# Start of a fused layer step: block 0's 1/rms from token rows, the first transfers in a new order, p's weights split once for two blocks

## The chip, the cores and the metric

The kernel runs on one core of one Trainium2 chip. The metric is the device time of one execution in microseconds (us), the median of three runs. The engines are TensorE (PE, with its weight loads as PEld), VectorE (DVE), ScalarE (ACT), GpSimd (POOL) and SyncE (SP). Each executes its own instructions strictly in the order in which they were built in; semaphores order the engines among themselves. SP, ACT and POOL issue DMA transfers.

## The reference, cut to what matters

One encoder layer over 2048 prompt tokens and 64 tokens of a sample stream, with model width 1024. Only what the start of the kernel computes is shown in full.

```python
h = rms_norm(x, g_pre)                       # x * 1/sqrt(mean(x*x) + 1e-6) * g_pre
proj = h @ w_in                              # 1024 -> ten groups of 1024
vA, bA, cA, zA, q, f, iv, zB, gA, gB = split_cols(proj)
...                                          # short convolution (path A), gated recurrence (path B)
merged = sigmoid(gA) * yA + sigmoid(gB) * yB
x = x + rms_norm(merged @ w_o, g_post)
gate = sigmoid(rms_norm(x, g_ple) @ w_ple_gate)
x = x + (p @ w_ple_proj) * gate              # p: 256 values per token
```

## The kernel before, in words

Activations lie feature-major: 128 features on the partitions, tokens along the free dimension. The 2112 tokens are worked on in three blocks of 704, each in two halves (`segs`) of 352.

A float32 product is put together from three matmuls of a rounded type. `split` (L183) makes the parts of a matrix: ScalarE casts it to the rounded type ("hi", L184), and VectorE subtracts that from the original ("lo", L185). Then hi by hi, hi by lo and lo by hi are added up in PSUM.

The projections go in groups of two column tiles (`sgroup`), each by a scheme of seven half-size products in place of eight. For it `combined` takes four weight tiles of `w_blk` (called A11, A21, A22, A12; 128x512, 256 KB each) and, in the first block, makes four sums and differences S3, S1, S2, S4 from them on VectorE (L281), splits A11, A12, A22 and the four sums, and stores low parts and sums in DRAM for later blocks. On the activation side `operands` (L604) takes x_fm rows in pairs, row i and row i+4, for i = 0 to 3 ("k"). It multiplies each with g_pre and 1/rms (L610), and makes seven operands from the pair by subtractions (L617, L618, L623, L624) and splits. The two first groups are those of `head_prep` for head 0: FF with QQ, then ZB with IV. `gates` (GA with GB) follows behind them.

`ple` computes p by w_ple_proj for one block. It goes over eight column tiles j, loads a piece of w_ple (128 KB), splits it, and does 12 matmuls of 128x352 (two halves, two row tiles of p, three parts). ScalarE copies each half out of PSUM (L922), and POOL's queue stores the tile. PSUM has three buffers for it. Pieces of weights share a pool: five buffers for raw tiles, four for hi, four for lo, three for sums. All larger activation tiles live in a ring of 52 slots of 128x704.

The start is in the last part of the program (L1078 to L1101). SP loads two tiles of p; POOL's queue loads the eight x_fm tiles and block 1's p; ScalarE's queue loads the small vectors. Then p is split; eight x_fm tiles are squared on ScalarE (L573, L576) and added up on VectorE (L577). `ple` of block 0 runs for six column tiles. 1/rms follows: column sums by matmuls with a column of ones (L558), scale and epsilon on VectorE (L530), the power -1/2 on POOL (L532), spreading over the partitions by matmuls with the identity (L542) and copies (L568). The rest of `ple`, the splits of block 1's p and the operands come next. Block 1's `ple` is handed to `gates` as a filler, two column tiles ahead of each of the four k steps of its first group.

The order on each engine is fixed when the program is built. The framework goes by program order and by a cost model; code under `tc.high_priority()` moves ahead of other work, and `tc.issue_after(ins)` holds what it covers back behind `ins`. A load that reuses a buffer waits for the readers of its former content.

Of the kernel before, what the change touches and what calls it, by code (L numbers as in the profile page):

```python
# [18 lines left out]
P = 128  # L19
# [63 lines left out]
def hybrid_step(  # L83
# [31 lines left out]
    def nm(s):  # L115
        uid[0] += 1
        return f"{s}_{uid[0]}"

    def rt(n=BN, dt=F32):
        t = ring.tile([P, BN + 4], dt, tag="r", name=nm("r"))  # L120
        return t if n is None else t[:, :n]
# [59 lines left out]


    def split(src, hi, lo):  # L183
        A.copy(hi, src)  # L184
        V.tensor_tensor(lo, src, hi.bitcast(F32), ALU.subtract)  # L185

    def split_rt(src):
        hi, lo = rt(dt=F32R), rt(dt=F32R)
        split(src, hi, lo)
        return hi, lo  # L190
# [34 lines left out]
    def load_w(idx):  # L225
# [5 lines left out]
                parts.append(split_w(raw, (idx, half_)))  # L231
        return parts

    last, hooks = [None], []

    def placed():
# [13 lines left out]
    def run(gen, n=None):  # L250
        for i, _ in enumerate(gen):
            if n is not None and i + 1 == n:
                break
# [17 lines left out]
    def combined(i1, i2, first, ahead):  # L271

        with tc.high_priority() if ahead else nullcontext():
            if not first:
                return {n: kept_w(i1, i2, n) for _, n, _, _, _ in PRODUCTS}
            a11, a21, a22, a12 = (load_raw(w_blk[i, h]) for i, h in ((i1, 0), (i2, 0), (i2, 1), (i1, 1)))
            out = dict(A11=split_w(a11, (i1, 0)))

            def total(name, x, y, op):
                s = sum_tile()  # L280
                V.tensor_tensor(s, x, y, op)  # L281
                out[name] = keep_sum(name, i1, s)
                return s

            total("S3", a11, a21, ALU.subtract)
            s1 = total("S1", a21, a22, ALU.add)
            s2 = total("S2", s1, a11, ALU.subtract)
            out["A12"] = split_w(a12, (i1, 1))
            out["A22"] = split_w(a22, (i2, 1))
            total("S4", a12, s2, ALU.subtract)  # L290
            return out
# [38 lines left out]
    def sgroup(i1, i2, hc, sink, first, mid=None, by_k=False, ahead=True, between=None):  # L330

        w = combined(i1, i2, first, ahead)
        ps, got = {}, {}

        def product(n, ks):
            bank, block, operand, start, _ = PRODUCTS[n]
            if bank not in ps:
                ps[bank] = ps_gemm()  # L340
            hi, lo = w[block]
            for k in ks:
                xhi, xlo = hc[operand][k]
                add = partial(T.matmul, ps[bank], skip_group_check=not start)
                add(hi[:, k, :], xhi, start=start and k == 0, stop=False)  # L345
                add(hi[:, k, :], xlo, start=False, stop=False)  # L346
                last[0] = add(lo[:, k, :], xhi, start=False, stop=k == KH - 1).ins  # L347

        if by_k:
            for k in range(KH):  # L350
                if between is not None:
                    between()
                for n in range(4):
                    product(n, (k,))
        for n, (bank, _, _, _, stop) in enumerate(PRODUCTS):
            if n >= 4 or not by_k:
                product(n, range(KH))
            if not stop:
                got[n] = hf()
                with tc.high_priority():  # L360
                    copied = A.copy(got[n], ps[bank])  # L361
                if n == 2 and mid is not None:
                    mid(copied.ins)
            if n == 3:
                u2 = got[0]
                V.tensor_tensor(u2, u2, ps["b"], ALU.add)
            elif n == 4:
                sink(0, 0, ps["a"], None)
            elif n == 5:
                sink(1, 0, u2, ps["c"])  # L370
                V.tensor_tensor(got[1], got[1], got[2], ALU.add)
                sink(1, 1, u2, got[1])
            elif n == 6:
                sink(0, 1, u2, ps["d"])
            hook()
# [186 lines left out]
    def rms(acc, out, segs):  # L562


        cols = [col_rstd(acc[:, cols_of(sg)], sg["n"]) for sg in segs]
        yield
        for sg, col in zip(segs, cols):
            A.copy(out[:, cols_of(sg)], spread(col, sg["n"]))  # L568
        yield

    def sum_squares(j, src, acc, n):
        if j == 0:
            A.activation(acc, src, AF.Square)  # L573
        else:
            sq = rt(n)
            A.activation(sq, src, AF.Square)  # L576
            V.tensor_tensor(acc, acc, sq, ALU.add)  # L577
# [23 lines left out]
                rstd_of(sc[:, 0:1], cols[:, i : i + 1], 1.0 / D)  # L601
            yield

    def operands(hc, rs, load):  # L604

        for i in range(KH):
            pair = []
            for k in (i, i + KH):
                xk = load(k)
                V.scalar_tensor_tensor(xk, xk, g_pre[:, k : k + 1], rs, ALU.mult, ALU.mult)  # L610
                pair.append(xk)
            (b11, b12), (b21, b22) = ([half(x, h) for h in range(2)] for x in pair)
            one = rt(dt=F32R)
            split(b11, half(one, 0), half(one, 1))
            hc["B11"].append((half(one, 0), half(one, 1)))
            s = rt()
            V.tensor_tensor(half(s, 1), b22, b12, ALU.subtract)  # L617
            V.tensor_tensor(half(s, 0), b12, b11, ALU.subtract)  # L618
            hi, lo = split_rt(s)
            hc["T3"].append((half(hi, 1), half(lo, 1)))  # L620
            hc["T1"].append((half(hi, 0), half(lo, 0)))
            t = rt()
            V.tensor_tensor(half(t, 0), b22, half(s, 0), ALU.subtract)  # L623
            V.tensor_tensor(half(t, 1), b21, half(t, 0), ALU.subtract)  # L624
            hi, lo = split_rt(t)
            hc["T2"].append((half(hi, 0), half(lo, 0)))
            hc["T4"].append((half(hi, 1), half(lo, 1)))
            hi, lo = split_rt(pair[1])
            hc["B21"].append((half(hi, 0), half(lo, 0)))
            hc["B22"].append((half(hi, 1), half(lo, 1)))  # L630
            yield
# [266 lines left out]


    def load_p(bl, queue):  # L900
        raws = [rt(), rt()]
        for k, raw in enumerate(raws):
            queue.dma_start(raw, p_fm[k * P : (k + 1) * P, bl["t0"] : bl["t0"] + BN])
        return raws

    def ple(bl, ph, kept):
        for j in range(KB):
            raw = wp.tile([P, 4, P], F32, tag="raw", name=nm("raw"), bufs=5)[:, :2, :]
            SP.dma_start(raw, w_ple[j])
            with tc.high_priority():  # L910
                hi = wp.tile([P, 4, P], F32R, tag="hi", name=nm("hi"))[:, :2, :]
                lo = wp.tile([P, 4, P], F32R, tag="lo", name=nm("lo"))[:, :2, :]
                split(raw, hi, lo)
            t = rt()
            for s in bl["segs"]:
                pp, c = ps_attn()[:, :HN], cols_of(s)
                for k, (xhi, xlo) in enumerate(ph):
                    T.matmul(pp, hi[:, k, :], xhi[:, c], start=k == 0, stop=False)
                    T.matmul(pp, hi[:, k, :], xlo[:, c], start=False, stop=False)
                    last[0] = T.matmul(pp, lo[:, k, :], xhi[:, c], start=False, stop=k == 1).ins  # L920
                with tc.high_priority():
                    A.copy(t[:, c], pp)  # L922
            kept["p", j] = spill("p", j)
            G.dma_start(kept["p", j], t)
            hook()
            yield
# [150 lines left out]

    kepts = [{} for _ in blocks]  # L1078
    ph = load_p(blocks[0], SP)
    A.dma_start(vec, vecs)  # L1080
    A.dma_start(hist_s, hist0)
    xs = []
    for k in range(KB):
        xs.append(rt())
        G.dma_start(xs[k], x_fm[k * P : (k + 1) * P, :BN])
    ph1 = load_p(blocks[1], G)
    ph = [split_rt(raw) for raw in ph]
    acc, rs = rt(), rt()
    for k, xk in enumerate(xs):
        sum_squares(k, xk, acc, BN)  # L1090
    first_ple, first_rms = ple(blocks[0], ph, kepts[0]), rms(acc, rs, blocks[0]["segs"])
    run(first_ple, 6)
    run(first_rms, 1)
    run(first_ple, 1)
    run(first_rms)
    run(first_ple)
    ph = [split_rt(raw) for raw in ph1]
    hc = new_operands()
    run(operands(hc, rs, lambda k: xs[k]))
    constants()  # L1100
    fills = gates(blocks[0], hc, kepts[0], True, steps(ple(blocks[1], ph, kepts[1]), 2))  # L1101
    for bi, bl in enumerate(blocks):
        first, kept = bi == 0, kepts[bi]
        segs = bl["segs"]
# [118 lines left out]
```

## Time and profile before

| | us |
|---|---|
| median of 3 runs (2727.76 to 2732.46) | 2730.09 |
| the profiled execution | 2728.34 |
| its span from first to last instruction | 2726.6 |
| mean granted TensorE clock in it | 0.987 of full speed |
| TensorE's first matmul | 13.30 |
| VectorE's first multiplication of x with 1/rms (L610) | 34.23 |
| first matmul of the first group (L345) | 37.78 |
| last matmul of block 0's ple | 35.58 (end) |
| block 1's ple, from and to | 97.69, 115.68 |

The page of the profile begins with the busy time of each engine. Below it the span is cut into 40 equal slices, each with the busy share in tenths, the granted TensorE clock (PEclk) and the DMA rate. Then come the DMA queues, the chain of work that ended last, and the costliest groups of instructions. The trace behind the page can be asked for a timeline (start, duration, engine, line, operation, tiles and shapes, and in brackets the idle time just before with the instruction that ended it), or for the busy time of each engine by stretch. "x3" on a row means that three instructions are drawn together. Engine times of one instruction overlap a little with the next, so spacing is shorter than duration.

### The profile page before, as it was taken

What the parts mean: (1) busy time and instruction counts of PE and PEld (TensorE: products, weight loads), DVE (VectorE), ACT (ScalarE), POOL (GpSimd) and SP (SyncE); (2) the same over time, 40 slices, a digit from 0 to 9 for tenths busy, and PEclk for the clock granted to TensorE, in tenths of its full rate; (3) what the DMA queues carried; (4) which work ended last, traced back from release to release, by engine and by line L of the source; (5) the groups of instructions that cost most, each with busy time, mean ns of one, the idle gap of its engine ahead of it and who ended that gap; (6) DMA issues with size and microseconds to landing.
All of it is one profiled execution on the core that took longest, in us unless ns stands there. A gap on an engine that the chain in (4) does not pass through costs nothing.

```text
span 2726.6 us, 47857 instructions
## 1 busy us (share of the span) xinstructions
PE 2646.6 (97%) x16736; PEld 2610.7 (96%) x16736; DVE 1721.8 (63%) x3327; ACT 1457.9 (53%) x2796; POOL 367.9 (13%) x684
## 2 busy tenths in 40 slices
PE   6999999999999999999999999999999999999998
PEld 5999999999999999999999999999999999999988
DVE  6788888899666643566645567554355554357864
ACT  4665565454324553566654556454466654445654
POOL 1000001100332211011111210021010010010022
PEclk7999999999999999999999999999999999999999
DMA  5767777898988898766789998598866678888878
GB/s 200 268 239 275 260 243 278 280 314 291 346 312 288 305 340 271 243 224 223 232 279 335 390 335 259 180 349 306 268 224 219 217 225 269 272 290 305 280 240 313
DMA packets 365681, 748.90 MB, mean 275 GB/s; under 512 B 44704, under 2 KB 48320, under 8 KB 365440
## 3 DMA queue, kind: packets, MB, share of 16 engines
q1 hardware_dynamic: 325728, 589.84, 64.9%
q0 software_dynamic: 39424, 155.96, 15.6%
q8 instruction: 132, 2.16, 0.3%
q14 instruction: 109, 0.89, 0.1%
q10 hardware_dynamic: 288, 0.05, 0.0%
HBM read 538.29 MB, written 207.37 MB: 273 GB/s over the span
## 4 chain that ended last, share of the span: by engine, by line
PE 78%; DMA 8%; DVE 4%; issue 4%; ACT 2%; POOL 1%; SPq 0%; DVEq 0%; POOLq 0%; ACTq 0%
PE pg L345 17%; PE pg L346 17%; PE pg L347 17%; PE pg L472 3%; PE pg L473 3%; PE pg L471 3%; PE pg L438 3%; PE pg L439 3%; PE pg L440 3%; DMA raw<-w_blk 2%; DMA raw<-S 1%; PE pa L826 1%; PE pa L862 1%; PE pa L864 1%; PE pa L816 1%
## 5 line engine op out<-in xcount | busy, mean ns | idle before, releaser
L345 PE MATMUL pg<-r,hi 128*128 128x352 f32 x3360 | 1115.1, 333 | 15.9 <-ACT r L184 5.9
L346 PE MATMUL pg<-r,hi 128*128 128x352 f32 x3360 | 1090.4, 325 | 5.0 <-DVE r L185 5.0
L347 PE MATMUL pg<-r,lo 128*128 128x352 f32 x2400 | 779.9, 325 | 4.8 <-DMA lo<-low 3.5
L215 ACT CAST hi<-raw 128x512 fp32r<-128x512 f32 x740 | 455.9, 619 | 589.7 <-PE pg L346 216.3
L345 PEld LDWEIGHTS pg<-r,hi 128*128 128x128 f32 x3360 | 634.8, 189 | 26.8 <-ACT r L184 8.9
L346 PEld LDWEIGHTS pg<-r,hi 128*128 128x128 f32 x3360 | 635.6, 189 | 9.6 <-DVE r L185 9.5
L347 PEld LDWEIGHTS pg<-r,lo 128*128 128x128 f32 x2400 | 454.0, 189 | 7.0 <-DMA lo<-low 4.7
L347 PE MATMUL pg<-r,s 128*128 128x352 f32 x960 | 310.5, 324 | 0.4 <-DMA s<-low 0.3
L472 PE MATMUL pg<-r,hi 128*128 128x352 f32 x896 | 291.9, 326 | 2.6 <-DVE r L185 2.3
L471 PE MATMUL pg<-r,hi 128*128 128x352 f32 x896 | 290.3, 326 | 1.8 <-ACT r L184 1.7
L473 PE MATMUL pg<-r,lo 128*128 128x352 f32 x728 | 237.5, 326 | 8.3 <-DVE lo L185 7.2
L184 ACT CAST r<-r 128x352 fp32r<-128x352 f32 (+2 forms) x294 | 162.8, 589 | 144.0 <-DVE r L962 43.3
L184 ACT CAST hi<-raw 128x512 fp32r<-128x512 f32 (+1 forms) x232 | 138.1, 597 | 181.2 <-PE pg L346 44.1
L185 DVE TENSOR_TENSOR r<-r,r 128x352 fp32r<-128x352 f32 (+2 forms) x294 | 183.6, 650 | 60.7 <-ACT r L184 60.0
L185 DVE TENSOR_TENSOR lo<-raw,hi 128x512 fp32r<-128x512 f32 (+1 forms) x232 | 152.2, 660 | 73.2 <-ACT hi L184 66.8
L438 PE MATMUL pg<-r,hi 128*128 128x352 f32 x560 | 182.6, 330 | 7.9 <-ACT r L184 7.9
L439 PE MATMUL pg<-r,hi 128*128 128x352 f32 x560 | 183.9, 330 | 0.9 <-DVE r L185 0.6
L347 PEld LDWEIGHTS pg<-r,s 128*128 128x128 f32 x960 | 180.4, 188 | 1.3 <-DMA s<-low 1.3
L472 PEld LDWEIGHTS pg<-r,hi 128*128 128x128 f32 x896 | 169.9, 190 | 4.5 <-DVE r L185 4.3
L184 ACT CAST hi<-s 128x512 fp32r<-128x512 f32 x160 | 98.8, 619 | 139.7 <-PE pg L346 137.0
L471 PEld LDWEIGHTS pg<-r,hi 128*128 128x128 f32 x896 | 169.6, 190 | 3.3 <-ACT r L184 2.9
L361 ACT COPY hf<-pg 128x352 f32<-128x352 f32 x360 | 158.3, 446 | 0.6
(327 smaller groups left out, 3991.7 us busy)
## 6 DMA issues: line engine op xcount, KB each, us to landing
raw<-w_blk SPq DMA_DIRECT2D x588, 256.0 KB, 4.0
lo<-low SPq DMA_DIRECT2D x422, 256.0 KB, 3.9
raw<-S SPq DMA_DIRECT2D x400, 256.0 KB, 4.0
low<-lo SPq DMA_DIRECT2D x344, 256.0 KB, 3.7
s<-low SPq DMA_DIRECT2D x318, 256.0 KB, 3.8
S<-s SPq DMA_DIRECT2D x160, 256.0 KB, 3.3
r<-x_fm POOLq DMA_DIRECT2D x40, 352.0 KB, 7.0
r<-w_blk POOLq DMA_DIRECT2D x48, 256.0 KB, 7.2
```

The costliest lines, as they stand in the source:

```text
L184: A.copy(hi, src)
L185: V.tensor_tensor(lo, src, hi.bitcast(F32), ALU.subtract)
L215: A.copy(hi, raw)
L345: add(hi[:, k, :], xhi, start=start and k == 0, stop=False)
L346: add(hi[:, k, :], xlo, start=False, stop=False)
L347: last[0] = add(lo[:, k, :], xhi, start=False, stop=k == KH - 1).ins
L361: copied = A.copy(got[n], ps[bank])
L438: add(hi[:, k, :], xhi, start=start and k == 0, stop=False)
L439: add(hi[:, k, :], xlo, start=False, stop=False)
L471: T.matmul(ps, hi[:, k % 4, :], xhi[:, c], start=k == 0, stop=False)
L472: T.matmul(ps, hi[:, k % 4, :], xlo[:, c], start=False, stop=False)
L473: last[0] = T.matmul(ps, lo[:, k % 4, :], xhi[:, c], start=False, stop=k == KB - 1).ins
```

## The change

* **1/rms of block 0** comes from token rows. Twelve tiles of x_tok (128 tokens by 512 features, 256 KB each) are loaded, three go with each of the first four column tiles of ple, and ScalarE squares each with a sum along its row. One addition on VectorE joins the two halves of a row. Scale, power and spreading follow on one 128x6 tile. The eight squares and seven additions of 128x704 and the column sums by matmuls go.
* **The first requests all stand on SP**: two tiles of p, w_ple 0 to 4, the twelve rows, x_fm in the order of the operands' pairs, then block 1's p. w_ple 5 to 7 are requested by POOL's queue.
* **p's splits** stand under high priority, ahead of those of w_ple.
* **w_ple's splits** are held in eight tiles of the ring (hi and lo side by side), and block 1's ple uses them instead of loading and splitting again.
* For the first five column tiles the second half is copied out of PSUM by VectorE instead of ScalarE.
* **`behind`** holds the weight splits and sums of the first group (FF with QQ) back behind the splits of block 1's p, and those of the second group behind the split of B21 at k=2 of the operands.
* The operands' first step (k=0) now stands ahead of the last column tiles of block 0's ple, and the splits of block 1's p behind these.

Lines of the changed kernel are some 3 to 43 further down than those of before.

```diff
@@ -181,8 +181,7 @@
 
 
     def split(src, hi, lo):
-        A.copy(hi, src)
-        V.tensor_tensor(lo, src, hi.bitcast(F32), ALU.subtract)
+        return A.copy(hi, src).ins, V.tensor_tensor(lo, src, hi.bitcast(F32), ALU.subtract).ins
 
     def split_rt(src):
         hi, lo = rt(dt=F32R), rt(dt=F32R)
@@ -231,6 +230,8 @@
                 parts.append(split_w(raw, (idx, half_)))
         return parts
 
+
+    behind = []
     last, hooks = [None], []
 
     def placed():
@@ -331,7 +332,10 @@
 
 
 
-        w = combined(i1, i2, first, ahead)
+        with ExitStack() as order:
+            for ins in behind.pop(0) if behind else ():
+                order.enter_context(tc.issue_after(ins))
+            w = combined(i1, i2, first, ahead)
         ps, got = {}, {}
 
         def product(n, ks):
@@ -601,7 +605,7 @@
                 rstd_of(sc[:, 0:1], cols[:, i : i + 1], 1.0 / D)
             yield
 
-    def operands(hc, rs, load):
+    def operands(hc, rs, load, marks=None):
 
         for i in range(KH):
             pair = []
@@ -625,7 +629,10 @@
             hi, lo = split_rt(t)
             hc["T2"].append((half(hi, 0), half(lo, 0)))
             hc["T4"].append((half(hi, 1), half(lo, 1)))
-            hi, lo = split_rt(pair[1])
+            hi, lo = rt(dt=F32R), rt(dt=F32R)
+            done = split(pair[1], hi, lo)
+            if marks is not None:
+                marks.append(done)
             hc["B21"].append((half(hi, 0), half(lo, 0)))
             hc["B22"].append((half(hi, 1), half(lo, 1)))
             yield
@@ -898,19 +905,34 @@
 
 
     def load_p(bl, queue):
-        raws = [rt(), rt()]
+        raws = [rt() for _ in range(2)]
         for k, raw in enumerate(raws):
             queue.dma_start(raw, p_fm[k * P : (k + 1) * P, bl["t0"] : bl["t0"] + BN])
         return raws
 
-    def ple(bl, ph, kept):
+    def load_ple(j, queue):
+        raw = wp.tile([P, 4, P], F32, tag="raw", name=nm("raw"), bufs=5)[:, :2, :]
+        queue.dma_start(raw, w_ple[j])
+        return raw
+
+    def ple(bl, ph, kept, raws=(), held=None, marks=None):
+
+
         for j in range(KB):
-            raw = wp.tile([P, 4, P], F32, tag="raw", name=nm("raw"), bufs=5)[:, :2, :]
-            SP.dma_start(raw, w_ple[j])
-            with tc.high_priority():
-                hi = wp.tile([P, 4, P], F32R, tag="hi", name=nm("hi"))[:, :2, :]
-                lo = wp.tile([P, 4, P], F32R, tag="lo", name=nm("lo"))[:, :2, :]
-                split(raw, hi, lo)
+            if held is not None and j in held:
+                hi, lo = held[j]
+            else:
+                raw = raws[j] if j < len(raws) else load_ple(j, G if held is not None else SP)
+                with tc.high_priority():
+                    if held is not None:
+                        both = rt(4 * P, F32R).rearrange("p (k c) -> p k c", c=P)
+                        held[j] = hi, lo = both[:, :2, :], both[:, 2:, :]
+                    else:
+                        hi = wp.tile([P, 4, P], F32R, tag="hi", name=nm("hi"))[:, :2, :]
+                        lo = wp.tile([P, 4, P], F32R, tag="lo", name=nm("lo"))[:, :2, :]
+                    done = split(raw, hi, lo)
+                if marks is not None:
+                    marks.append(done)
             t = rt()
             for s in bl["segs"]:
                 pp, c = ps_attn()[:, :HN], cols_of(s)
@@ -919,7 +941,10 @@
                     T.matmul(pp, hi[:, k, :], xlo[:, c], start=False, stop=False)
                     last[0] = T.matmul(pp, lo[:, k, :], xhi[:, c], start=False, stop=k == 1).ins
                 with tc.high_priority():
-                    A.copy(t[:, c], pp)
+                    if marks is not None and j < 5 and s is bl["segs"][1]:
+                        V.tensor_copy(t[:, c], pp)
+                    else:
+                        A.copy(t[:, c], pp)
             kept["p", j] = spill("p", j)
             G.dma_start(kept["p", j], t)
             hook()
@@ -1077,28 +1102,46 @@
 
     kepts = [{} for _ in blocks]
     ph = load_p(blocks[0], SP)
+    ple_raws = [load_ple(j, SP) for j in range(5)]
     A.dma_start(vec, vecs)
     A.dma_start(hist_s, hist0)
-    xs = []
-    for k in range(KB):
-        xs.append(rt())
-        G.dma_start(xs[k], x_fm[k * P : (k + 1) * P, :BN])
-    ph1 = load_p(blocks[1], G)
-    ph = [split_rt(raw) for raw in ph]
-    acc, rs = rt(), rt()
-    for k, xk in enumerate(xs):
-        sum_squares(k, xk, acc, BN)
-    first_ple, first_rms = ple(blocks[0], ph, kepts[0]), rms(acc, rs, blocks[0]["segs"])
-    run(first_ple, 6)
-    run(first_rms, 1)
+    rows = []
+    for s in blocks[0]["segs"]:
+        for _, o in tiles_of(HN):
+            for q in range(2):
+                rows.append(rt(512))
+                SP.dma_start(rows[-1], x_tok[s["t0"] + o : s["t0"] + o + P, q * 512 : q * 512 + 512])
+    xs = {}
+    for k in (k for i in range(KH) for k in (i, i + KH)):
+        xs[k] = rt()
+        SP.dma_start(xs[k], x_fm[k * P : (k + 1) * P, :BN])
+    ph1 = load_p(blocks[1], SP)
+    with tc.high_priority():
+        ph = [split_rt(raw) for raw in ph]
+    held, marks = {}, []
+    first_ple = ple(blocks[0], ph, kepts[0], ple_raws, held, marks)
+
+    ss = small.tile([P, 2, 6], F32, tag="rows", name="rows", bufs=1)
+    for i, t in enumerate(rows):
+        if i % 3 == 0:
+            run(first_ple, 1)
+        with tc.issue_after(marks[-1][0]):
+            A.activation(t, t, AF.Square, accum_out=ss[:, i % 2, i // 2 : i // 2 + 1])
+    with tc.issue_after(marks[-1][1]):
+        V.tensor_tensor(ss[:, 0, :], ss[:, 0, :], ss[:, 1, :], ALU.add)
+    rstd_of(ss[:, 0, :], ss[:, 0, :], 1.0 / D)
     run(first_ple, 1)
-    run(first_rms)
+    rs = spread_all([ss[:, 0, :3], ss[:, 0, 3:]])
+    hc = new_operands()
+    ops = operands(hc, rs, lambda k: xs[k], behind)
+    run(ops, 1)
     run(first_ple)
-    ph = [split_rt(raw) for raw in ph1]
-    hc = new_operands()
-    run(operands(hc, rs, lambda k: xs[k]))
+    ph = [(rt(dt=F32R), rt(dt=F32R)) for _ in ph1]
+    after_p = [split(raw, *hl) for raw, hl in zip(ph1, ph)][-1]
+    run(ops)
+    behind[:] = after_p, behind[2]
     constants()
-    fills = gates(blocks[0], hc, kepts[0], True, steps(ple(blocks[1], ph, kepts[1]), 2))
+    fills = gates(blocks[0], hc, kepts[0], True, steps(ple(blocks[1], ph, kepts[1], (), held), 2))
     for bi, bl in enumerate(blocks):
         first, kept = bi == 0, kepts[bi]
         segs = bl["segs"]
```

## The prediction

> **What bounds the kernel now.** First the engine table of the page: TensorE is busy 97% of the span, so the end moves only with work taken from TensorE or with time in which it stands still. The sliced rows then say where it stands still.
>
> ```profile
> PE 2646.6 (97%) x16736; PEld 2610.7 (96%) x16736; DVE 1721.8 (63%) x3327; ACT 1457.9 (53%) x2796; POOL 367.9 (13%) x684
> ...
> PE   6999999999999999999999999999999999999998
> ...
> PEclk7999999999999999999999999999999999999999
> ```
>
> Only the first slice (68 us) shows a hole and a low clock, and it is the stretch that the change touches. I therefore read the start by stage.
>
> ```profile
> 0.00:13.30 13.30, 0.00 (x1) 0.00 (x1) 4.64 (x24) 3.95 (x9) 6.75 (x17) 1.00 0.87 302
> 13.30:20.00 6.70, 5.58 (x18) 5.08 (x18) 6.03 (x8) 6.70 (x12) 0.00 (x0) 1.00 0.75 265
> ...
> 37.80:50.00 12.20, 6.64 (x15) 3.84 (x15) 12.14 (x19) 2.65 (x5) 0.00 (x0) 0.55 0.35 126
> 50.00:64.00 14.00, 10.72 (x25) 6.34 (x24) 10.04 (x17) 6.20 (x11) 0.00 (x0) 0.50 0.00 0
> 64.00:70.00 6.00, 5.96 (x20) 5.58 (x21) 3.83 (x7) 2.95 (x6) 0.00 (x0) 0.52 0.28 93
> 70.00:97.70 27.70, 27.12 (x168) 26.52 (x166) 26.51 (x48) 21.38 (x36) 0.00 (x0) 1.00 0.72 247
> ```
>
> Columns: stretch, its length, busy us (instructions) of PE, PEld, DVE, ACT and POOL, granted clock, DMA share, GB/s. Three stages have three limits. Until 13.3 TensorE waits for p's casts. From 37.8 to 64 VectorE is nearly full (12.14 of 12.20) or alternates with ScalarE, and TensorE does 40 matmuls in 26 us at half clock: VectorE, making the operands, sets the pace. From 70 TensorE is dense. So an earlier start of TensorE is worth nothing by itself; what counts is **when the operand stage ends**, and how many matmuls are left behind it. The timeline gives the anchors.
>
> ```profile
> 13.30 1.25 PE L918 MATMUL pa<-r,hi 128*128 128x352 f32 x3 [13.30 <-ACT r L184]
> 34.23 1.81 DVE L610 SCALAR_TENSOR_TENSOR r<-r,vec,r 128x704 f32<-128x704 f32 x2
> 37.78 0.43 PE L345 MATMUL pg<-r,hi 128*128 128x352 f32 x1 [2.20 <-ACT r L184]
> 40.23 0.66 PE L346 MATMUL pg<-r,hi 128*128 128x352 f32 x1 [2.01 <-DVE r L185]
> 111.46 0.43 PE L920 MATMUL pa<-r,lo 128*128 128x352 f32 x1 [0.54 <-DVE lo L185]
> 113.96 0.43 PE L920 MATMUL pa<-r,lo 128*128 128x352 f32 x1 [0.29 <-DVE lo L185]
> 115.68 0.32 PE L346 MATMUL pg<-r,hi 128*128 128x352 f32 x1
> ```
>
> VectorE's first operand (L610, x times 1/rms) starts at 34.23. Block 1's ple ends on TensorE at 115.68; from there the order of TensorE's instructions is the same in both kernels. So the question is how far 115.68 moves.
>
> **Unit costs**, as spacing of back-to-back instructions in the timelines: VectorE 128x704 0.81, with a scalar operand (L610) 0.86, 128x512 0.60, 128x352 0.43, 128x256 0.34; ScalarE cast 128x704 0.69, 128x512 0.52, 128x256 0.31, PSUM copy 0.34; ScalarE square with accumulation 128x512 0.61 (L599, two in a row at 471.73 and 472.34); a 128x352 matmul 0.161 at full clock, 0.29 at half.
>
> **Step 1, the new 1/rms.** Before, it needs all eight x_fm rows, eight ScalarE squares of 0.70, seven VectorE adds of 0.81 and the 128x1 matmuls, and is ready at 34.2. After: p's casts can start when the lbt exponential has run, about 5.1 (4.84 plus 0.21 before), and end at 6.5; TensorE's first matmul comes at about 6.9. SP requests p and five w_ple (1.4 MB), then 12 rows (3.1 MB). At 0.36 MB/us (the sliced DMA rate of the start shows 315 to 408 GB/s between 2.5 and 17.5) the first 1.4 MB are in at about 6.8, as 2.5 + 1.4/0.36 + some 0.4, and the last row 3.1/0.36 = 8.7 later, at 15.5. ScalarE is later than that: per column tile one cast, three squares and one copy, 0.31 + 3 x 0.61 + 0.34 = 2.5, four times from 6.9 gives 16.9, and waits for TensorE's half clock (3.5 per tile in the first 5.2 us, as from 13.30 to 18.50) bring the last square to 18.1. The power on POOL over 128x6 is not in the trace: 128x3 took 0.90, 128x4 1.09, so 0.9 if the size did not count and 1.9 in proportion; I take 1.4. Done at about 20.0. The six spreading matmuls stand behind tile 4's products (20.9 to 22.2, 1.50 for 12 before), the two copies end at 22.65. First operand at **22.7, 11.5 earlier**. The DVE copies that replace five ScalarE copies (0.43 each, 2.2) fall into 8 to 22, where VectorE has little else: nothing, and 2.2 without that cover.
>
> **Step 2, what VectorE must do then.** The static order of after puts behind the first operand what before had done ahead of it: the splits of w_ple 5 to 7 (3 x 0.34), and of the first group's weights four sums and three splits (7 x 0.60), and one sum of the second group (0.60): 5.8. The rest is the same work. Head start left: 5.7.
>
> **Step 3, the waits that take its place.** VectorE executes in order, and in after the subtracts for w6, w7, p of block 1 and A11 stand in a row ahead of three quarters of the operands. Each needs a ScalarE cast, and ScalarE's casts are queued behind evacuations: w6's cast behind tile 5's first copy, w7's behind two more, p's first behind another two. The evacuations need TensorE, which has been idle from 22.2 to 31.95 (w5's cast stands behind the cast of k=0's fourth operand) and so runs cold at 0.29. In turn: lo of w5 done at 33.8; the rest of tile 5's first half 1.5, copy 0.45, cast 0.4: lo of w6 starts 36.0 (VectorE has had nothing since 34.6: 1.4 lost); 12 matmuls, copy and cast: lo of w7 39.55 (3.2 lost); lo of p 42.2 (2.3 lost). Sum 6.9. The S4 sum waits for the store of S3, whose buffer it takes (store 3.3 to 5.5): 0.3 more. 11.5 - 5.8 - 6.9 - 0.3 = **-1.5: the operand stage ends 1.5 later** than before, though it starts 11.5 earlier. The transfers in this stage hide: the last x_fm lands at about 23, p at 25, A11 at 28, all ahead of their readers.
>
> **Step 4, what TensorE gains.** (a) 18 of block 1's 96 ple matmuls now stand in the operand stage instead of behind it: 18 x 0.161 = 2.9 less, if TensorE's idle time there covers them; uncovered they cost their 2.9 and the gain is nothing. (b) The stalls of 0.54 and 0.29 on splits of block 1's w_ple go, since the split halves are kept: 0.8; next late there is nothing, as 70 to 97.7 is dense. The removed eight loads (1 MB), casts (8 x 0.31) and subtracts (8 x 0.34) lay beside dense TensorE work: nothing. The extra 3.1 MB lies in a start that has no later claimant for 20 us: nothing, 8.7 if it did all fall on the path (3.1 MB at 0.36). The six fewer matmuls are 128x1 columns under 0.12 each, off the path.
>
> **Sum.** +1.5 - 2.9 - 0.8 = -2.2. The profiled execution took 2728.34 (span 2726.6 and 1.7 around it), so 2726.1; it lies 1.75 below the median of 2730.09, so against the median **2727.9**. A difference under about 0.2% (5.5 us) can hardly be told from none by a measurement of this kernel; this one is 0.08%.
>
> **Rivals.**
>
> *The clock stays up* (faster). If the 18 extra matmuls and tiles 5 to 7 keep TensorE warm, two pieces go: the cold ple chain of step 3 (about 21 matmuls on the path to p's casts, each 0.13 shorter, less what the casts still take: 2.0) and the cold re-entry, where 64 to 70 holds 20 matmuls and 6.0 / 0.161 = 37 would fit: 17 x 0.161 = 2.7. -2.2 - 4.7 = -6.9, 2723.2. Against it: before, the clock fell to half within the 4.9 us from 35.3 to 40.2, in gaps of 2.20 and 2.01 with one matmul of 0.43 between, and after leaves longer gaps. [...]
>
> *The head start survives* (faster). If TensorE, ScalarE and VectorE interleave better than I chained them, because w5 to w7 are cast while VectorE is in k=0, the 6.9 of waits go: -9.1, 2721.0. For it: in before the same casts wait only 0.35 for TensorE. Against it: the order is fixed and in it each cast stands behind a copy.
>
> *The rows come late* (slower). One SP queue now carries all first transfers; before, SP and POOL shared them at 302 GB/s until 13.3. If SP alone gives R MB/us, the last row lands at about 2 + 4.5/R, and the first operand 7.2 later. The time is that of before at a first operand of 24.9, and slower by 5.5 at 30.4, so R of 0.21; at 0.19 it is 33 and +8, 2738. Against it: SP's queue moved 589.84 MB in 64.9% of 16 engines' time, 333 GB/s at full share. [...]
>
> That the change does not do what it says is excluded by the instructions: eight splits fewer, twelve loads of rows more.
>
> **Chances.** Forecast 0.46, clock 0.27, head start 0.13, late rows 0.14. Faster by over 0.2% 0.40, within 0.46, slower 0.14. The forecast alone, with the power's 0.5 either way, the 18 matmuls uncovered (+2.9) and a tile of cold products more or less (1.7), is 2725 to 2732. Over the cases, leaving out 1 in 10 on each side: the head start with half of the clock's gain is 2718.5, so 2718 at the low end; late rows at 0.19 is 2738 at the high end.
>
> **What would show it.** TensorE's first matmul near 7; the first operand near 22.7 (each us later is a us lost); VectorE idle about 7 us between 34 and 44 on ScalarE casts of w_ple and p (none: the head start survived); the granted clock between 32 and 70 (above 0.6: the clock rival); the first matmul after block 1's ple near 113.5. The prediction fails if VectorE is not the limit of the operand stage any more, or if a transfer ends a wait there.

## The result, and the profile after

The changed kernel takes 2725.72 us (median of 15 runs, 2722.06 to 2731.99) where the kernel before takes 2731.28 beside it. The ratio is 0.998 (0.997 to 0.9989). Two more comparisons gave 0.999 (0.9979 to 1.000) and 0.9984 (0.9975 to 0.9993), and the kernel before against itself 1.0004 (0.9994 to 1.0013). The mean of the three is 0.9985, **4.2 us faster**; three intervals of 0.001 either way make it some 1.6 either way. The forecast was 2.2.

The sliced rows of after, in the same columns as those of before (stretch, length, busy us of PE, PEld, DVE, ACT and POOL, granted clock, DMA share, GB/s):

```profile
0.00:6.90 6.90, 0.16 (x1) 0.17 (x1) 4.13 (x21) 3.24 (x6) 1.38 (x7) 1.00 0.73 220
6.90:13.30 6.40, 5.14 (x16) 4.24 (x17) 1.83 (x4) 3.75 (x12) 0.91 (x2) 1.00 0.95 314
13.30:20.00 6.70, 6.67 (x30) 6.08 (x30) 1.80 (x4) 5.76 (x20) 2.35 (x5) 1.00 1.05 407
20.00:30.00 10.00, 4.50 (x30) 3.88 (x28) 6.50 (x13) 3.56 (x9) 2.48 (x4) 0.84 1.03 410
30.00:37.80 7.80, 2.43 (x7) 1.98 (x8) 7.13 (x11) 1.77 (x3) 0.00 (x0) 0.50 0.26 89
37.80:50.00 12.20, 11.52 (x60) 10.43 (x58) 6.16 (x11) 6.71 (x14) 2.24 (x5) 0.89 0.59 197
50.00:64.00 14.00, 9.62 (x24) 5.57 (x24) 10.40 (x19) 5.84 (x9) 0.00 (x0) 0.65 0.41 144
64.00:70.00 6.00, 4.00 (x11) 3.09 (x12) 5.09 (x9) 1.67 (x4) 0.00 (x0) 0.50 0.52 173
```

TensorE now works from 6.7 on, and VectorE has little to do up to 20. But from 37.8 to 50, where VectorE was full before (12.14 of 12.20), it now works for 6.16: it waits. TensorE stands still from 24.7 to 34.4. (The clock column shows 1.00 up to 16.6 only because the record of the clock begins there: until 16.5 the matmuls follow each other at 0.29 us, as they do in the stretches recorded at 0.50; from 16.7 on it is 0.16.) VectorE's timeline of after names the waits (start, duration, and in brackets the idle time before, with what ended it):

```profile
25.22 1.82 DVE L614 SCALAR_TENSOR_TENSOR r<-r,vec,r 128x704 f32<-128x704 f32 x2 [1.30 <-ACT r L553]
...
38.69 0.43 DVE L184 TENSOR_TENSOR r<-raw,r 128x256 fp32r<-128x256 f32 x1 [1.56 <-ACT r L184]
41.88 0.42 DVE L184 TENSOR_TENSOR r<-raw,r 128x256 fp32r<-128x256 f32 x1 [2.76 <-ACT r L184]
44.55 1.93 DVE L184 TENSOR_TENSOR r<-r,r 128x704 fp32r<-128x704 f32 x2 [2.25 <-ACT r L184]
```

The first operand comes at 25.22 (34.23 before), and then 1.56 + 2.76 + 2.25 = 6.57 us go in waits for the casts of w_ple 6 and 7 and of block 1's p.

All kernels share a marker just behind the start: the first transpose of head 0's attention on TensorE. It is at 121.32 and 122.25 in two profiles of before (mean 121.8), and at 120.55, 120.63 and 118.80 in three of after (mean 120.0). The first row is before, the second after:

```profile
121.32 0.60 PE L804 MATMUL pa<-ident,r 128*128 128x128 f32 x4
```
```profile
120.55 0.60 PE L811 MATMUL pa<-ident,r 128*128 128x128 f32 x4
```

So the start is worth 1.8 us by the means; profiles of one kernel differ by up to 1.8 at this marker, so this is known to about 1 us. **About half of the 4.2 us comes from elsewhere**: what that is stands behind the experiments.

### The profile page after: what moved, and what is told of

It is laid out like the page before. It is cut to its first block, busy times and chain, and to the rows that moved or that the text cites. A ratio compares the mean times of both kernels' runs of the same rounds, so it can differ in the third digit from the quotient of the medians.

```text
span 2723.2 us, 47794 instructions
## 1 busy us (share of the span) xinstructions
PE 2643.2 (97%) x16724; PEld 2608.4 (96%) x16724; DVE 1713.4 (63%) x3317; ACT 1455.4 (53%) x2799; POOL 364.5 (13%) x676
## 4 chain that ended last, share of the span: by engine, by line
PE 81%; DMA 6%; issue 5%; DVE 3%; POOL 1%; ACT 1%; DVEq 0%; POOLq 0%; SPq 0%; ACTq 0%
PE pg L349 18%; PE pg L351 18%; PE pg L350 18%; PE pg L442 3%; PE pg L476 3%; PE pg L443 3%; PE pg L477 3%; PE pg L444 3%; PE pg L475 3%; DMA raw<-w_blk 2%; PE pa L833 1%; PE pa L869 1%; PE pa L871 1%; PE pa L823 1%; DMA r<-p 1%
## 5 line engine op out<-in xcount | busy, mean ns | idle before, releaser
L184 ACT CAST hi<-raw 128x512 fp32r<-128x512 f32 (+1 forms) x216 | 131.6, 611 | 165.0 <-PE pg L350 39.5
L184 DVE TENSOR_TENSOR lo<-raw,hi 128x512 fp32r<-128x512 f32 (+1 forms) x216 | 145.1, 676 | 65.2 <-ACT hi L184 47.2
```

The lines of the kernel that those rows point to most:

```text
L184: return A.copy(hi, src).ins, V.tensor_tensor(lo, src, hi.bitcast(F32), ALU.subtract).ins
```

## The experiments

| kernel | first operand | marker | ratio to before |
|---|---|---|---|
| before, twice | 34.2, 35.4 | 121.3, 122.3 | 1.0004 |
| after, three times | 25.2, 25.0, 23.7 | 120.6, 120.6, 118.8 | 0.998, 0.999, 0.9984 |
| operands behind block 0's ple | 24.3 | 116.1 | 0.9974 (0.9963 to 0.9985) |
| w_ple split again | 24.9 | 124.5 | 0.9996 (0.9985 to 1.0006) |
| weights not held back | 35.5 | 127.2 | |
| before, with kept splits alone | 37.0 | 120.6 | |
| TensorE kept at work | 23.6 | 118.0 | |
| squares first | 25.3 | 122.9 | |
| block 1's p earlier | 24.0 | 115.6 | |
| after, block 1's ple in the stage | 25.0 | 112.3 | |
| the last two together | 23.5 | 104.2 | 0.9933 (0.9921 to 0.9946) |

First operand and marker are in us. The kernels without a ratio were executed once beside before; at differences of a few us such a single time tells nothing, so they are read by the marker alone.

### Before against itself, and after twice more

No edit.

> This is the kernel before, unchanged, against itself. Both theories expect a ratio of 1.000; how far the interval reaches tells what five rounds can tell apart. It also gives a second profiled execution of before. Theory A (the change is worth what its start is worth, about 1 us in the one pair of profiles: block 1's ple ends at 114.4 in place of 115.7; the rest of the 5.6 us between the medians is the clock, which falls for single windows of 3.4 us at places that differ between two executions of one kernel): two profiles of before differ from each other by 2 to 4 us behind 120 us, and by under 1 us ahead of it. Theory B (the change also moves the later part of the kernel, by some 3 to 5 us): the two profiles of before agree within 1 us at every point, and differ from after behind 120 us.

> This is the changed kernel, unchanged, on another chip job. Theory A: the ratio to before is 0.9990 to 0.9997 (1 to 2.5 us faster), and the second profile of after differs from its first by 2 to 4 us behind 120 us, in both directions. Theory B: the ratio is 0.998 again (5 to 6 us), and both profiles of after gain at the same places behind 120 us.

> The changed kernel a third time, unchanged. Its start is worth 1.2 us by the shared marker (120.6 against a mean of 121.8), while the two comparisons gave ratios of 0.998 and 0.999. Theory A (the rest is where single windows of 3.4 us at half clock happen to fall): a ratio of 0.9995, with an interval that may hold anything from 0.9985 to 1.0005, and the marker at 120.6 again. Theory B (something behind 120 us gains 3 to 4 us): a ratio near 0.998.

Measured: 1.0004, 0.999 and 0.9984. Neither theory holds as it stood. Profiles of one kernel differ by some 6 us behind the marker, more than the 2 to 4 of A; but the mean of the three ratios is 4.2 us from 1, and the 1.8 us of the start lie outside 4.2 plus or minus 1.6, if not by much. Something behind the marker seems to gain too.

### Operands behind block 0's ple

```diff
-    run(ops, 1)
     run(first_ple)
```

> After, but the operands' first step stands behind the last column tiles of block 0's ple, not ahead of them. Then the casts of w_ple 5 to 7 and of block 1's p no longer stand behind the cast of k=0's fourth operand, and TensorE goes on to tiles 5 to 7 at once. If the waits of VectorE on these casts (1.56 + 2.76 + 2.25 = 6.6 us in after's trace, at 38.7, 41.9 and 44.6) are what ate the head start, they go: the operand stage ends 4 to 6.6 us earlier than in after and the kernel takes 4 to 6 us less than after (ratio to before about 0.9975 by theory A, 0.996 by theory B). The rival: the stage is bound by VectorE's work and by the alternation with ScalarE whatever the order, and the waits only move to k=0's operands: within 1.5 us of after.

The marker came 4.5 us ahead of the two profiles of after known then (116.11), 3.9 ahead of the mean of all three. The ratio is 0.9974, some 3 us better than after's mean, which the intervals alone could hardly tell from nothing. The waits on w_ple are nearly gone: the three splits now stand around the first multiplications of x, with 0.93, 0 and 0.24 us of waiting. The head start was eaten by the order in which VectorE meets these casts. Another wait takes their place. ScalarE's timeline of this kernel:

```profile
31.79 0.78 ACT L184 CAST r<-r 128x704 fp32r<-128x704 f32 x1 [1.35 <-DMA r<-p_fm]
...
33.64 0.78 ACT L184 CAST r<-r 128x704 fp32r<-128x704 f32 x1 [0.72 <-DMA r<-p_fm]
```

Block 1's p, requested last but for the weights, lands at 31.8 and 33.6.

### w_ple split again for block 1

```diff
-steps(ple(blocks[1], ph, kepts[1], (), held), 2)
+steps(ple(blocks[1], ph, kepts[1]), 2)
```

> After, but block 1's ple loads and splits w_ple again, as before the change. In its order all 96 matmuls of block 1's ple stand behind head 0's products. By the prediction's step 4 the 18 matmuls that no longer stand in the operand stage cost 18 x 0.161 = 2.9 us, and the stalls on the splits 0.8: 3.7 us slower than after. If the matmuls in the operand stage were not covered (they hold up ScalarE and VectorE there), it is 0.8 us slower or less.

The marker: 124.54, 3.9 us later than 120.6. The sum of step 4 (2.9 + 0.8) holds at the marker. Behind the operand stage the price is larger: from the end of the last operand's first subtractions (L622) to the marker it is 58.1 here and 53.2 to 53.7 in after, so 4.7; the stage itself ends some 0.4 us sooner without the 18 matmuls, counted from the first operand, and the first operand came 0.3 us earlier in this run. The whole time tells more: by the marker this kernel is 2.7 us slower than before, but the ratio is 0.9996. That is again some 3 us that the start doesn't show.

### Weights not held back

```diff
-    behind[:] = after_p, behind[2]
+    behind.clear()
```

> After, without the holding back of the weights' splits and sums. Read by a marker that all kernels share, the first transpose of head 0's attention on TensorE: 121.32 and 122.25 us in the two profiles of before, 120.55 and 120.63 in those of after, so that single looks tell 1 us apart. In the order of this kernel the split of A11 and the sum S3 stand ahead of the first operand on VectorE, and A11 is requested last on SP (at 22.2, landed near 32 in after). If VectorE's fixed order is what counts, the first operand waits for that landing: from 25.2 to 32 or later, and since some of the sums then fill the later waits, the marker comes 3 to 5 us later than in after. The rival: the sums fill the 6.6 us of waits and the kernel gains: the marker 3 to 4 us earlier.

The first theory in direction, more in size: the marker at 127.16, 6.6 us later than in after. VectorE stands at the split of A11:

```profile
32.91 0.69 DVE L184 TENSOR_TENSOR lo<-raw,hi 128x512 fp32r<-128x512 f32 x1 [11.22 <-ACT hi L184]
```

ScalarE waited 11.09 us for A11 to land at 32.26, and the copies of 1/rms stood behind that cast (33.12 and 34.96). So the holding back is a part that the change needs, since it has put the weights last on SP.

### Kept splits alone, in the kernel before

The diff's part on `held` (eight tiles of the ring, reused by block 1's ple), applied to before; w_ple is still loaded on SP as before.

> Before, with one part of the change alone: the split w_ple is kept for block 1. Its order puts 15 of block 1's matmuls into the operand stage, as in after. If this part is worth the same in both surroundings (undoing it in after cost 3.9 us at the marker: 124.54 against 120.6), the marker comes 3 to 4 us earlier than in before, at 117.5 to 119. The rival: the kept part only gains because after leaves TensorE idle around 33 to 50 us; in before, whose TensorE is idle there as well, it must gain, so a gain under 1 us would say that the price of undoing it in after came from something else, such as the additional loads.

The marker: 120.60, only 0.7 to 1.7 ahead of before. The order on VectorE changed with it: the first operand comes at 36.98 (34.2 and 35.4 before), and a sum then waits for a store of S whose buffer it takes:

```profile
36.98 1.81 DVE L610 SCALAR_TENSOR_TENSOR r<-r,vec,r 128x704 f32<-128x704 f32 x2
40.83 0.69 DVE L281 TENSOR_TENSOR s<-raw,raw 128x512 f32<-128x512 f32 x1 [2.04 <-DMA S<-s]
```

From the first operand to the marker it is 83.6, against 87.1 and 86.9 in before: behind the first operand the kept splits save 3.4 us here too, and 1.6 to 2.8 of it is lost ahead of it. So a part of a change need not have the same price in both surroundings where a fixed order is planned anew around it.

### TensorE kept at work

```diff
+    xw, pw = ph[0][0], ps_attn()[:, :HN]
+    for _ in range(48):
+        T.matmul(pw, held[0][0][:, 0, :], xw[:, :HN], start=True, stop=True)
     hc = new_operands()
```

> After, with 48 additional matmuls on TensorE, whose result is not used, behind the spreading of 1/rms: they fill the idle time from 24.7 to about 32.5. If an idle TensorE is what brings the clock down there (it stands at half from 26.9 to 40.6 in after), the clock stays up, the matmuls of block 0's last ple tiles take 0.16 in place of 0.29, and the chain of casts up to block 1's p ends 2.0 us earlier (the price of the clock rival): marker at 118.6. The rival: the chain is paced by the copies and casts on ScalarE, so that a faster TensorE only waits longer: less than 0.7 us.

Inconclusive on the price of the clock. The additional matmuls ended at 31.0, TensorE idled 1.77 and 0.96 us ahead of the first real ones, and the clock fell for 3.4 us from 35.2 on all the same (0.78 in the row below). The marker is at 117.95, but 1/rms was early in this run: from the first operand to the marker it is 94.4, against 95.3, 95.6 and 95.1 in the three profiles of after. So the chain gained 0.7 to 1.2 of the 2.0 us that the clock rival put on it, in a run where the clock did not stay up.

```profile
32.00:34.20 2.20, 0.91 (x4) 0.62 (x4) 2.20 (x3) 0.75 (x2) 0.00 (x0) 1.00 0.04 14
34.20:42.00 7.80, 7.25 (x32) 6.54 (x32) 2.13 (x5) 3.16 (x8) 1.08 (x2) 0.78 0.45 132
```

### Squares first

On top of the operands behind block 0's ple: the twelve squares are chained under high priority behind the first cast of w_ple, and the spreading stands behind column tile 1.

> The version with the operands behind block 0's ple (marker 116.11), with the twelve squares chained ahead of ScalarE's copies and the spreading behind column tile 1 in place of 4: 1/rms should come 3 to 4 us earlier (first operand at about 21 in place of 24.25). If the first operand sets the end of the stage, the marker comes 3 to 4 us earlier, near 113. If not the first operand but the landing of block 1's p does (ScalarE waits for it until 31.8 and 33.6 there), the marker moves by less than 1 us.

It missed what it was made for: the squares ended at 18.9, but the first operand came at 25.26, since the power reached TensorE only at 21.81 and the spreading then ran at half clock (2.93 us for the twelve matmuls, 1.50 before; the next ones are 0.29 apart). The last six ple tiles were left behind it, and w7 and p again came late: the marker is at 122.93. What an earlier 1/rms is worth stays open.

### Block 1's p earlier, and block 1's ple in the operand stage

```diff
     for k in (k for i in range(KH) for k in (i, i + KH)):
+        if k == 2:
+            ph1 = load_p(blocks[1], SP)
         xs[k] = rt()
...
-    run(ops)
+    next_ple = ple(blocks[1], ph, kepts[1], (), held)
+    for _ in range(KH):
+        run(ops, 1)
+        run(next_ple, 2)
```

The first edit is made on the version with the operands behind block 0's ple; the second is made on that, and by itself on after. `gates` then gets no filler.

> The version with the operands behind block 0's ple, with block 1's p requested ahead of the last four x_fm tiles on SP. If the landing of block 1's p is what VectorE waits for at 31.8 and 33.6 there, the casts of p come at about 30 and 31 and the marker (first transpose of head 0's attention) moves from 116.11 to 114 or 114.5. The rival: the last x_fm tiles, now 0.7 MB later (1.7 us at 0.41 MB/us), take its place as the wait: the marker within 0.5 us of 116.1.

> The same as the last, and all of block 1's ple stands between the steps of the operands, in place of 18 matmuls there and 78 behind head 0's products. If TensorE's time in the operand stage is free (step 4 of the prediction: a matmul moved there is worth 0.161 us), the marker comes up to 78 x 0.161 = 12.6 us earlier than in that version, less what its 16 copies on ScalarE (0.34 each, 5.4 in all) hold up: 102 to 108, and the ratio to before 0.993 to 0.995. The rival: ScalarE alternates with VectorE there, the copies come between, and the stage ends later by what the matmuls save: marker 112 to 116, ratio 0.997.

> The changed kernel, with nothing else than block 1's ple between the steps of its operands. By the same sum the marker moves from 120.6 to between 108 and 113; by the rival it stays at 118 or later.

The earlier p alone moved the marker by 0.5 (115.59), less than forecast, and not because of the x_fm tiles: the landing of A11 took p's place as the wait (the cast of A11 waits 1.47 us for it, until 33.42). Block 1's ple in the stage moved it by 11.4 more, to 104.17, and by 8.3 in after (112.27). So the sum of step 4 nearly applies to all of block 1's ple: 11.4 of the 12.6 us of 78 matmuls. TensorE's time in the operand stage is almost free. Two sliced rows of 50 to 70, first of the version with p earlier, then with block 1's ple in the stage:

```profile
50.00:70.00 20.00, 15.76 (x50) 11.50 (x50) 14.61 (x25) 9.25 (x16) 0.00 (x0) 0.58 0.26 80
```
```profile
50.00:70.00 20.00, 19.57 (x118) 18.93 (x118) 16.28 (x27) 12.30 (x24) 2.46 (x6) 0.98 0.46 167
```

118 matmuls in place of 50, and VectorE's last operand (L627) starts at 65.39 in place of 64.67. With TensorE at work the clock is up too (0.98 in place of 0.58); how much of the 11.4 us is the clock's was not tried apart. This version takes **2713.18 us, ratio 0.9933 (0.9921 to 0.9946)**, 18 us less than before.

### Where the other three microseconds come from

This was read from the traces, and no run tests it. I compared times between VectorE instructions that all kernels share. From 1504 to 1588 us (block 1's path A and merge), the three profiles of the kernels with before's start take 2.6, 4.0 and 3.1 us more than after; the eleven with after's start differ from each other by 0.5 at most. Mean to mean that is 3.1. Nearly all of it arises within 3 us, from 1585.5 to 1588.5 in after, at VectorE's subtractions for the splits of w_blk. One of the three is the kernel with kept splits alone, so keeping the splits is not what gains here. POOL's timeline there, of before and then of after:

```profile
1573.33 0.54 POOL L931 DMA_DIRECT2D r<-g__2815_11256  x1
1573.87 0.54 POOL L931 DMA_DIRECT2D r<-g__2816_11258  x1
1574.40 0.54 POOL L931 DMA_DIRECT2D r<-g__2852_11421  x1
```
```profile
1573.79 0.54 POOL L956 DMA_DIRECT2D r<-g__2783_11203  x1
1576.85 0.54 POOL L956 DMA_DIRECT2D r<-g__2784_11205  x1 [2.52 <-ACT hi L214]
1577.38 0.54 POOL L956 DMA_DIRECT2D r<-g__2820_11368  x1
```

POOL requests the reload of the gate tiles. In after it pauses 2.52 us behind the first. The instruction in the bracket is only inferred, and hardly the cause: in after the request behind POOL's 113th, 219th, 325th and 431st, each 106 apart, comes 3.07, 3.08, 3.07 and 2.95 us after it, and behind the 219th and the 431st the profile names nothing that was waited for. The two requests that follow above are 0.53 apart. In before the four distances are 3.79, 5.80, 3.31 and 19.24. The change takes 7 requests from POOL's queue (514 in before, 507 in after: x_fm's eight and two of p go to SP, three of w_ple come), so the 325th, at 1545 in before beside a wait that POOL had anyway, is now the first gate reload. The pause of 2.52 us at that place is in all eleven profiles with after's start and in none of the three with before's. What it moves are seven reloads of 352 KB, away from SP's loads of w_blk, for which ScalarE's casts wait at the end of path A. From 1565 to 1592 these loads land 8.0 us after their request in before and 6.3 in after (medians of nine). ScalarE in before:

```profile
1589.03 0.62 ACT L184 CAST hi<-raw 128x512 fp32r<-128x512 f32 x1 [3.35 <-DMA raw<-w_blk]
...
1591.24 0.62 ACT L184 CAST hi<-raw 128x512 fp32r<-128x512 f32 x1 [0.85 <-DMA raw<-w_blk]
...
1595.93 0.62 ACT L184 CAST hi<-raw 128x512 fp32r<-128x512 f32 x1 [3.33 <-DMA raw<-w_blk]
```

and in after only one of the three waits:

```profile
1593.27 0.62 ACT L184 CAST hi<-raw 128x512 fp32r<-128x512 f32 x1 [3.22 <-DMA raw<-w_blk]
```

With 3.1 us for this place and the marker for the start, the sums are: after 1.8 + 3.1 = 4.9 faster (measured 4.2), operands behind ple 5.7 + 3.1 = 8.8 (7.1, between 4.1 and 10.1), w_ple split again 2.7 slower - 3.1 = 0.4 faster (1.1), the last version 17.6 + 3.1 = 20.7 (18.3, between 14.7 and 21.6). They agree within the intervals. That the pause gains the 3.1 us, and not another difference of the two starts, is argued from these rows and not shown: no kernel changed the number of POOL's requests alone.

## Why the prediction was right, point by point

The time, the direction and the likeliest case were right, but three errors stand behind the 2.2 us: a later first operand (slower), a clock that came back sooner (faster), and a gain at a place that the prediction did not look at (faster). The first two nearly cancel: that the start alone, 1.8 us, comes so near to 2.2 is luck. The third makes the whole gain nearly twice the forecast.

* **"What bounds the kernel" and the extra work of 5.8**: right. VectorE's fixed order sets the stage: TensorE's first matmul came 6.6 us earlier (6.74), the marker 1.8.
* **Step 1, "first operand at 22.7"**: wrong by 1 to 2.5 (25.2, 25.0, 23.7). ScalarE's first square waited for its row until 9.55, 2.87 us; the sum had taken the chain from 6.9 on and counted no wait for rows. TensorE's half clock was in the sum with 1.2 us, and cost about that: the two column tiles behind the first took 2.97 and 3.17 rather than 2.5. From the first operand on a delay goes through to the marker: the distance is 95.3, 95.6 and 95.1 in the three profiles.
* **Step 3, "sum 6.9"** for the waits: 6.57, at the three places named. "The operand stage ends 1.5 later" was more: the last operand's first subtractions (L622 in after, L618 before) end at 67.2 and 63.1. That is 4.1 later, and 1.5 + 2.5 from step 1 is 4.0. (By the means of all profiles the first operand is 10.2 earlier and the stage ends 2.9 later, which fits as well.) "The transfers in this stage hide" was right for after by luck: p landed between 30 and 32 and A11 at 31.9, not at 25 and 28, and as soon as the order was better, they were the wait.
* **Step 4, "2.9" and "0.8"**: 3.9 together at the marker, by the kernel that splits again. But a stage that ends 2.9 later and 3.7 from this step would bring the marker only 0.8 earlier, and it came 1.8 earlier. From the end of the stage to the marker it is 58.2 and 58.0 in before, 58.1 with w_ple split again, and 53.2 to 53.7 in after: 4.7 less, not 3.7. The clock goes with the rest: full speed returns 3.9 to 4.1 us behind the end of the stage in after, and 6.5 to 7.1 in those three profiles. At half clock the matmuls followed each other at 0.29 us, at full clock at 0.161, so 2.6 us less of it are worth up to 2.6 x (1 - 0.161 / 0.29) = 1.2, as an estimate. No run shows this alone.
* **"So the question is how far 115.68 moves"** is the step that failed: the order of instructions behind it is the same, the time isn't. Behind the marker 3.1 us of the answer arose, most likely by the count of POOL's requests.
* **The rivals.** The head start did not survive, and could have: taking one line out gained some 4 us at the marker. The rows came late, but the first operand by 1.0 to 2.5 us only, not near the 30.4 at which that rival is 5.5 slower. The clock did something between the forecast and its rival: it stood at half from 26.9 to 40.5 and from 54.2 to 71.2, and at full speed between, while the last two tiles of ple and the 18 matmuls ran. Of the rival's two pieces the first hardly showed (6.57 of waits for 6.9), and the second (2.7) came in part, as said under step 4.

## What to carry to other kernels

Where an engine's order is fixed, an earlier input is worth only what the first late instruction in that order leaves of it: look for the casts and copies that stand in a row, and ask which engine releases each. Work of the engine that is the bound of the whole kernel belongs into the stage where another engine sets the pace; here 78 matmuls moved there gained 11.4 us at the marker, the start of the whole change 1.8. And a measured gain should be looked for where the profile shows it: two traces, aligned on instructions that they share, told that a good half of it was at a place that the diff does not touch.

## What the runs showed of the hardware

* In after POOL's requests pause behind the 113th, 219th, 325th and 431st, each 106 apart: 3.07, 3.08, 3.07 and 2.95 us from request to request, where the next two behind the 325th are 0.53 apart. In before the distances at the same four are 3.79, 5.80, 3.31 and 19.24. Behind the 7th, another 106 earlier, there was no pause in before (0.54). What causes the pause and what ends it is not in the trace.
* The recorded stretches at half clock in before and after (but for the last of each profile, which its end cuts off) last 3.41, 6.83, 10.24, 13.65, 17.07 or 30.72 us: all multiples of 3.41. Behind the marker 38.8 us are at half clock in before and 27.0 in after. In two profiles of one kernel the places partly differ: in before the clock is at half from 1595.6 to 1605.8, and in the second execution of that kernel not at all from 1590 to 1600 (granted clock 1.00; 0.66 from 1600 to 1610). Over twelve executions of the kernel before, the mean clock was between 0.984 and 0.989, with times of 2735.87 and 2726.00 us.
* In before the clock fell at 39.1, where the 3.4 us ahead hold one matmul of 0.43 between gaps of 2.20 and 2.01, and with TensorE kept at work it fell at 35.2, behind gaps of 1.77 and 0.96. So in these two it fell without a gap of more than 2.20 us just ahead.
* With SP requesting nearly all, 407 to 410 GB/s moved from 13.3 to 30, with the 16 DMA engines busy all the time (a share of 1.03 to 1.05): that SP made nearly all the requests was not the limit there.
